# Block products of a GLA and SwiGLU layer: the last of four sums of raw weights made by an accumulating DMA instead of VectorE

## The chip, the core and the metric

The kernel runs on one core of a Trainium2 chip. The core has five engines that run their own instruction streams and wait for each other through semaphores: TensorE (PE, the matrix products; its weight loads are shown as PEld), VectorE (DVE), ScalarE (ACT), GpSimd (POOL) and SyncE (SP, which here only issues DMAs). DMAs issued by SP go through the hardware queue q1, those issued by GpSimd through the software queue q0; both are carried by the same 16 DMA engines. The metric is the device time of one execution in microseconds (us).

## The reference

One layer with 512 tokens and width 2048, in float32. Only the first kind of mixer is used (a gated linear attention, GLA), then a SwiGLU:

```python
h = rms_norm(x, norm_g[0, 0])
y = gla_mixer(h, w_in, w_a2, b_a, g_norm, w_out)   # 4 heads, ends in o @ w_out, w_out 2048 x 2048
x = x + y
x = x + swiglu(rms_norm(x, norm_g[0, 1]), w_gu, w_down)

def swiglu(h, w_gu, w_down):                       # w_gu 2048 x 11264, w_down 5632 x 2048
    g, u = split(h @ w_gu, 2)
    return (silu(g) * u) @ w_down
```

The change concerns the three last products, o @ w_out, h @ w_gu and (silu(g) * u) @ w_down.

## The kernel before, in words

**Split operands.** A float32 operand is split into hi (a rounded copy, made by ScalarE) and lo (what is left, made by VectorE), and a product is three matmuls: hi x hi, hi x lo, lo x hi (L1096 to L1098).

**Block products.** The three last products are made in the manner of Strassen and Winograd: a 2 x 2 block product takes seven products instead of eight, with sums of blocks on both sides. The activations' sums ("forms", seven a chunk: e0, e1, e2, l1, l0, e3, l2) are made once, split, and kept in DRAM or on chip; their tiles on chip are named fe and fl. The weights' sums are made on the fly from raw blocks of 256 x 512 (a tile of 128 x 1024, 512 KB): B11 (slot 0), B12 (slot 1), B22 and later B21 (both slot 2).

**Groups, phases, jobs.** The work is a list of 21 groups: groups 0 and 1 for w_out, groups 2 to 12 for w_gu, groups 13 to 20 for w_down. Each group has 2 to 4 chunks of the inner dimension and seven phases, one for each form; a job is one phase of one chunk, 12 matmuls. PHASES (L651) gives for each phase the form, the slot of the weights that is split, the bank that the product is added to, and the sum that is made first:

```python
("e0", 0, "x", None), ("e1", 0, "y", (0, 1, 0)), ("e2", 0, "x", (0, 0, 2)),
("l1", 2, "y", (1, 2, 1)), ("l0", 1, "x", None), ("e3", 2, "z", (0, 0, 2)), ("l2", 0, "x", None)
```

So phase 1 makes slot 0 = slot 1 - slot 0, phase 2 slot 0 = slot 0 - slot 2, phase 3 slot 1 = slot 2 - slot 1, and phase 5, once slot 2 holds B21, slot 0 = slot 0 + slot 2; that is what phase 6 multiplies. All four sums are made by VectorE (L687). Phases 0, 1, 2 and 6 read slot 0, phase 4 slot 1, phases 3 and 5 slot 2.

**Order.** The order on each engine is that in which the program emits its instructions. `run_job(m)` (L1070) emits the sum of job m + 3 (`add_stage`), the split of job m + 2 (`split_stage`: hi by ScalarE L696, lo by VectorE L697, into a pool of three buffers), the 12 matmuls of job m, and then what is due at m. `split_stage` also emits the loads into the buffers that a split has freed: at phase 3 the load of B21 (blk 3), at phases 4, 5 and 6 the three first loads of the next group (L675, all on SP). Among what is due (`at(m, ...)`) are, one job after a phase's last, the `take` functions that fetch the finished banks, and the form loads (L582, on SP).

**Groups 0 and 1.** `take_out` (L896) starts its sums s, v and u at phases 0, 1 and 2: ScalarE copies the bank to a tile (L915) and GpSimd issues an accumulating DMA of 256 KB that adds the residual x from DRAM to it (L916; two each, one for each half of 256 tokens). VectorE adds the later banks: to u at phase 3's take (L918), to v at phase 4's (L921), to s at phase 5's (L926); L918 is due with the first job of phase 4. GpSimd's queue also holds the stores of finished sums (L906), of forms (L603, L828), and in the down groups the loads of the residual (L1054), whose addition (L1058) is emitted three jobs later. In group 0 the forms of the last head are not ready before the group starts: the forms l1, l0 and l2 are loaded while it runs (`late_loads`, L748), the four of l0 are emitted at jobs 11 to 14, and phase 4 begins with job 16. Group 1 uses the same forms again, which are then on chip. Of the forms of group 2, those of two chunks are stored by GpSimd to DRAM (xF, L828) during groups 0 and 1 and loaded by SP in group 1; the others are made in place.

Of the kernel before, what the change touches and what calls it, by code (L numbers as in the profile page):

```python
# [11 lines left out]
ALU = mybir.AluOpType  # L12
PSUM = bass.MemoryType.PSUM

P = 128
# [9 lines left out]
G = 512  # L25
# [11 lines left out]
def f32(ap):  # L37
    return ap.bitcast(F32)
# [3 lines left out]
def trunk_kernel(ctx: ExitStack, tc: tile.TileContext, x, xT, cst, masks, wa2r, w_in, w_out, w_gu, w_down, out):  # L42
    nc = tc.nc
# [21 lines left out]
    def mis_bank():  # L65
        return mis_ps.tile([P, G], F32, tag="mis", name="mis")
# [161 lines left out]
    b = mis_bank()  # L228
# [352 lines left out]
    def load_form(src, f, c):  # L581
        nc.sync.dma_start(f32(form_tile(f, c % 4)), src[c][:, MADE.index(f)])  # L582
# [48 lines left out]
    def early_load(c):  # L631
# [15 lines left out]
    groups = [(w_out, range(4), (2 * p * G, (2 * p + 1) * G)) for p in range(2)]  # L647
    groups += [(w_gu, range(4) if fg else (0, 1, 3, 2), (fg * G, FF + fg * G)) for fg in range(N_FG)]
    groups += [(w_down, chunks, (2 * p * G, (2 * p + 1) * G)) for p, chunks in DOWN]

    PHASES = (  # L651
        ("e0", 0, "x", None),
        ("e1", 0, "y", (0, 1, 0)),
        ("e2", 0, "x", (0, 0, 2)),
        ("l1", 2, "y", (1, 2, 1)),
        ("l0", 1, "x", None),
        ("e3", 2, "z", (0, 0, 2)),
        ("l2", 0, "x", None),
    )
    jobs = [(g, ph, j) for g in range(len(groups)) for ph in range(7) for j in range(len(groups[g][1]))]  # L660
# [3 lines left out]
    w_at = {}  # L664

    def load(g, blk, j):

        if g >= len(groups) or j >= len(groups[g][1]):
            return
        src, chunks, cols = groups[g]  # L670
        slot = min(blk, 2)
        t = rw.tile([P, 2, G], F32, tag=f"r{(slot + g) % 3}{j}", name="raw")
        k0 = 4 * chunks[j] + (2 if blk > 1 else 0)
        n0 = cols[0] if blk in (0, 3) else cols[1]
        nc.sync.dma_start(t, src[k0 * P : (k0 + 2) * P, n0 : n0 + G].rearrange("(c p) f -> p c f", p=P))  # L675
        w_at[g, slot, j] = t
# [3 lines left out]
    def add_stage(m):  # L680
        if m >= len(jobs) or m in added:
            return
        added.add(m)
        g, ph, j = jobs[m]
        if (op := PHASES[ph][3]) is not None:
            to, a, b = (w_at[g, slot, j] for slot in op)
            (nc.vector.tensor_add if ph == 5 else nc.vector.tensor_sub)(to, a, b)  # L687

    def split_stage(m):
        if m >= len(jobs):  # L690
            return
        g, ph, j = jobs[m]
        raw = w_at[g, PHASES[ph][1], j]
        hi = wp.tile([P, 2, G], F32R, tag="hi", name="hi")
        lo = wp.tile([P, 2, G], F32R, tag="lo", name="lo")
        nc.scalar.copy(hi, raw)  # L696
        nc.vector.tensor_sub(lo, raw, f32(hi))  # L697
        ahead.append((hi, lo))
        split_done.append(m)
        if ph == 3:  # L700
            load(g, 3, j)
        elif ph > 3:
            load(g + 1, ph - 4, j)
            if j == len(groups[g][1]) - 1:
                for k in range(j + 1, 4):
                    load(g + 1, ph - 4, k)
# [13 lines left out]
    x1d = dram.tile([P, 4, D], F32, name="x1d")  # L720

    split_stage(0)
    split_stage(1)
    add_stage(4), add_stage(5)
    last = gate(3, banks)
    split_stage(2)
    ps.close()
    zz_ps = ffn.enter_context(tc.tile_pool(name="zz_ps", bufs=1, space=PSUM, reuse_waits="tile"))
# [15 lines left out]
    def at(m, fn):  # L744
        due.setdefault(m, []).append(fn)
# [221 lines left out]
    for n in range(2):  # L967
        for ph, k in enumerate((18, 18, 19, 19, 20, 22, 26)):
            at(first_of[1, 0] + k + n, lambda f=PHASES[ph][0], n=n: load_form(xF, f, n))

# [71 lines left out]
    def plan_loads():  # L1042
        seen = set()
        for d, (_, chunks) in enumerate(DOWN):
            for i, c in enumerate(c for c in chunks if c not in seen):
                seen.add(c)
                for ph in range(7):
                    at(first_of[D0 + d - 1, ph] + i + 1, lambda f=PHASES[ph][0], c=c: load_form(hF, f, c))

# [20 lines left out]
    def run_job(m):  # L1070
        nonlocal XYZ, keep
        g, ph, j = jobs[m]
        f, _, q, _ = PHASES[ph]
        chunks = groups[g][1]
        if j == 0:
            if ph == 0:
                XYZ, keep = dict(first_banks) if g == 0 else {}, {}
            if q not in XYZ:
                pr = banks_of["xyz".index(q)]
                XYZ[q] = [bank(f"q{pr}{i}") for i in range(2)]  # L1080
        add_stage(m + 3)
        while len(split_done) <= min(m + 2, len(jobs) - 1):
            split_stage(len(split_done))
# [94 lines left out]
```

## Time and profile before

| | us |
|---|---|
| median of 3 timed runs | 2079.57 (2078.95 to 2079.61) |
| the profiled execution, its own time | 2081.49 |
| its span in the trace | 2079.7 |
| TensorE busy in it | 2065.5 |
| VectorE, ScalarE, GpSimd busy | 1601.7, 938.7, 313.5 |
| mean granted TensorE clock | 0.997 |

The profile names an instruction by engine, line of the kernel and tiles, as out<-in. In a row of a group, the numbers behind the bar are its busy time in us and the mean of one in ns, and behind the second bar the idle time of the engine just before it and what ended that. A row of the timeline has the start and the length in us. A row of the waits has the total, the number of times and the longest. A row of busy time by windows has the length and then, for each engine, the busy time and the number of instructions, then granted clock, share of the 16 DMA engines that is busy (the shares of packets can add up to a little over 1) and GB/s. A row of a DMA queue has packets, MB and the share of the 16 engines' time in the window asked for. A "DMA to landing" is the time from the issue of a DMA to the semaphore that tells that its data are there.

### The profile page before, as it was taken

How to read it: one execution, taken by the hardware profiler on the slowest of the kernel's cores; microseconds unless marked ns; L12 is line 12 of the kernel's file. 1: busy time of each engine (PE TensorE's matmuls, PEld its weight loads, DVE VectorE, ACT ScalarE, POOL GpSimd, SP SyncE). 2: the span in 40 equal slices, each digit the busy share in tenths (PEclk: the TensorE clock that was granted, in tenths of full speed). 3: DMA queues.
4: the chain of work that ended last, by engine and by line, in shares of the span. 5: the costliest groups of instructions: out<-in, count | busy, mean ns of one | idle time of the engine just before them, and what ended most of it. 6: DMA issues, size and time to landing. Idle time of an engine off the chain costs nothing.

```text
span 2079.7 us, 24526 instructions
## 1 busy us (share of the span) xinstructions
PE 2065.5 (99%) x9314; PEld 1713.0 (82%) x9314; DVE 1601.7 (77%) x1778; ACT 938.7 (45%) x1165; POOL 313.5 (15%) x315
## 2 busy tenths in 40 slices
PE   9999999999999999999999999999999999999999
PEld 7887888888887887888888888888888888888887
DVE  7856566665448799788788788788788787888887
ACT  6343334333334556545445445445445454333333
POOL 6324242423111120011011011011011010000000
PEclk9999999999999999999999999999999999999999
DMA  6222222224784885553553553553555676675632
GB/s 212 76 83 68 78 71 81 82 77 129 261 310 141 320 264 211 164 177 114 173 178 114 174 177 114 175 177 115 173 176 167 223 278 243 223 273 194 233 136 100
DMA packets 161333, 350.22 MB, mean 168 GB/s; under 512 B 14400, under 2 KB 30912, under 8 KB 161216
## 3 DMA queue, kind: packets, MB, share of 16 engines
q1 hardware_dynamic: 136704, 274.76, 40.9%
q0 software_dynamic: 21440, 71.84, 10.2%
q10 hardware_dynamic: 3072, 2.06, 0.3%
q8 instruction: 73, 1.20, 0.2%
q14 instruction: 44, 0.36, 0.1%
HBM read 279.93 MB, written 68.68 MB: 168 GB/s over the span
## 4 chain that ended last, share of the span: by engine, by line
PE 94%; DVE 4%; ACT 1%; POOL 0%; issue 0%; DMA 0%; SPq 0%; DVEq 0%; ACTq 0%; POOLq 0%
PE bank L1097 22%; PE bank L1098 22%; PE bank L1096 22%; PE acc L134 8%; PE acc L133 8%; PE acc L135 7%; PE mis L427 2%; PE bank L791 1%; DVE lo L697 1%; DVE raw L687 1%; PE mis L485 1%; PE mis L135 0%; PE mis L133 0%; PE mis L134 0%; DVE qt L392 0%
## 5 line engine op out<-in xcount | busy, mean ns | idle before, releaser
L696 ACT CAST hi<-raw 128x1024 fp32r<-128x1024 f32 x518 | 544.5, 1054 | 684.7 <-PE bank L1098 574.9
L697 DVE TENSOR_TENSOR lo<-raw,hi 128x1024 fp32r<-128x1024 f32 x518 | 631.5, 1223 | 202.0 <-ACT hi L696 199.3
L1097 PE MATMUL bank<-lo,fe 128*128 128x512 f32 x1184 | 462.5, 391 | 2.7 <-DVE lo L697 2.6
L1096 PE MATMUL bank<-hi,fe 128*128 128x512 f32 x1184 | 464.2, 392 | 0.1
L1098 PE MATMUL bank<-hi,fe 128*128 128x512 f32 x1184 | 462.1, 390 | 0.0
L687 DVE TENSOR_TENSOR raw<-raw 128x1024 f32<-128x1024 f32 x296 | 361.0, 1220 | 2.7 <-DMA raw<-w_down 2.4
L1096 PE MATMUL bank<-hi,fl 128*128 128x512 f32 x888 | 345.7, 389 | 0.0
L1098 PE MATMUL bank<-hi,fl 128*128 128x512 f32 x888 | 345.5, 389 | 0.0
L1097 PE MATMUL bank<-lo,fl 128*128 128x512 f32 x888 | 345.5, 389 | 0.0
L1097 PEld LDWEIGHTS bank<-lo,fe 128*128 128x128 f32 x1184 | 222.8, 188 | 51.6 <-DVE lo L697 6.3
L1098 PEld LDWEIGHTS bank<-hi,fe 128*128 128x128 f32 x1184 | 222.7, 188 | 46.6
L1096 PEld LDWEIGHTS bank<-hi,fe 128*128 128x128 f32 x1184 | 222.7, 188 | 46.0 <-ACT hi L696 0.5
L122 DVE TENSOR_TENSOR lo<-raw,hi 128x1024 fp32r<-128x1024 f32 (+1 forms) x97 | 124.0, 1286 | 166.1 <-ACT hi L121 153.4
L133 PE MATMUL acc<-x,hi 128*128 128x512 f32 x512 | 202.9, 396 | 0.5 <-ACT x L170 0.5
L134 PE MATMUL acc<-x,hi 128*128 128x512 f32 x512 | 199.6, 390 | 0.3 <-DVE x L171 0.3
L135 PE MATMUL acc<-x,lo 128*128 128x512 f32 x512 | 199.7, 390 | 0.1
L121 ACT CAST hi<-raw 128x1024 fp32r<-128x1024 f32 (+1 forms) x97 | 100.6, 1040 | 213.1 <-PE acc L134 144.1
L1097 PEld LDWEIGHTS bank<-lo,fl 128*128 128x128 f32 x888 | 166.7, 188 | 35.5
L1096 PEld LDWEIGHTS bank<-hi,fl 128*128 128x128 f32 x888 | 166.7, 188 | 35.1 <-issue 0.3
L1098 PEld LDWEIGHTS bank<-hi,fl 128*128 128x128 f32 x888 | 166.7, 188 | 34.2
L828 POOL DMA_DIRECT2D hF<-hh x44 | 33.0, 749 | 788.3 <-ACT hs L818 691.9
L133 PEld LDWEIGHTS acc<-x,hi 128*128 128x128 f32 x512 | 96.2, 188 | 21.3 <-issue 1.0
(208 smaller groups left out, 2105.2 us busy)
## 6 DMA issues: line engine op xcount, KB each, us to landing
raw<-w_gu SPq DMA_DIRECT2D x176, 512.0 KB, 4.2
raw<-w_down SPq DMA_DIRECT2D x88, 512.0 KB, 5.4
raw<-w_in SPq DMA_DIRECT2D x64, 512.0 KB, 3.9
fe<-hF SPq DMA_DIRECT2D x44, 512.0 KB, 5.9
fl<-hF SPq DMA_DIRECT2D x33, 512.0 KB, 6.6
raw<-w_out SPq DMA_DIRECT2D x32, 512.0 KB, 8.5
raw<-w_in SPq DMA_DIRECT2D x62, 256.0 KB, 3.2
gF<-st POOLq DMA_DIRECT2D x48, 256.0 KB, 5.3
```

What stands on the lines that cost most here:

```text
L121: nc.scalar.copy(hi[:, c], raw[:, c])
L122: nc.vector.tensor_sub(lo[:, c], raw[:, c], f32(hi[:, c]))
L133: nc.tensor.matmul(out, ah, bh, start=start, stop=False)
L134: nc.tensor.matmul(out, ah, bl, start=False, stop=False)
L135: nc.tensor.matmul(out, al, bh, start=False, stop=stop)
L427: nc.tensor.matmul(bk[:, g * w : (g + 1) * w], kt[:, c, gg * P : (gg + 1) * P], qt[:, o : o + w], start=c == 0, stop=c == 1,)
L687: (nc.vector.tensor_add if ph == 5 else nc.vector.tensor_sub)(to, a, b)
L696: nc.scalar.copy(hi, raw)
L697: nc.vector.tensor_sub(lo, raw, f32(hi))
L1096: nc.tensor.matmul(o, ah, bh, start=a and begin, stop=False, skip_group_check=True)
L1097: nc.tensor.matmul(o, ah, bl, start=False, stop=False, skip_group_check=True)
L1098: nc.tensor.matmul(o, al, bh, start=False, stop=z, skip_group_check=True)
```

## The change

The fourth sum is no longer made by VectorE. When `split_stage` emits the split of phase 3 and the load of B21 into slot 2, it now also emits, on GpSimd's queue, a DMA that reads the same B21 block from DRAM once more and adds it to slot 0 in place (`accum_op=ALU.add`). Phase 5 keeps its split of B21 and its products, and has no sum in PHASES any more, so `add_stage` issues only subtractions.

```diff
-        ("e3", 2, "z", (0, 0, 2)),
+        ("e3", 2, "z", None),
...
-            (nc.vector.tensor_add if ph == 5 else nc.vector.tensor_sub)(to, a, b)
+            nc.vector.tensor_sub(to, a, b)
...
         if ph == 3:
             load(g, 3, j)
+            src, chunks, cols = groups[g]
+            k0 = 4 * chunks[j] + 2
+            nc.gpsimd.dma_start(
+                w_at[g, 0, j],
+                src[k0 * P : (k0 + 2) * P, cols[0] : cols[0] + G].rearrange("(c p) f -> p c f", p=P),
+                accum_op=ALU.add,
+            )
```

There are 74 such DMAs of 512 KB, one for each chunk of each group.

## The prediction

> **What bounds the kernel now.** First the page's busy times, the DMA row of the 40 slices and the group of the step that is moved.
>
> ```profile
> PE 2065.5 (99%) x9314; PEld 1713.0 (82%) x9314; DVE 1601.7 (77%) x1778; ACT 938.7 (45%) x1165; POOL 313.5 (15%) x315
> DMA  6222222224784885553553553553555676675632
> L687 DVE TENSOR_TENSOR raw<-raw 128x1024 f32<-128x1024 f32 x296 | 361.0, 1220 | 2.7 <-DMA raw<-w_down 2.4
> ```
>
> TensorE is busy 99% of a span of 2079.7 us: 14.2 us of idle time are left, in the whole kernel. VectorE, which the change relieves, is at 77%. So the next view is who waits for whom, kept to TensorE: does it ever wait for VectorE?
>
> ```profile
> PE mis L427 <- DVE qt L400: 5.3, 4, 3.0
> PE bank L1097 <- DVE lo L697: 2.6, 3, 1.6
> ```
>
> The first row is the attention stage, which the change leaves alone. In the block products TensorE waits for VectorE's splits three times, 2.6 us together. That is the most that a lighter VectorE can give back there.
>
> The third view is busy time by windows. The first two lie in the first block product group (group 0); the next two are around the largest of the three waits; then the gate/up groups, and one group of the down projection.
>
> ```profile
> 666.00:667.30 1.30, 1.30 (x7) 1.09 (x6) 1.30 (x2) 0.54 (x1) 0.00 (x0) 1.00 0.05 9
> 667.30:687.00 19.70, 19.70 (x88) 16.06 (x86) 14.17 (x14) 9.57 (x13) 2.90 (x4) 1.00 0.99 320
> 645.40:647.50 2.10, 0.55 (x2) 0.24 (x2) 2.10 (x3) 1.59 (x3) 0.00 (x0) 1.00 0.00 0
> 647.50:651.00 3.50, 3.50 (x9) 2.77 (x10) 3.47 (x5) 2.54 (x5) 2.38 (x3) 0.51 0.27 43
> 760.00:1600.00 840.00, 839.30 (x3790) 694.28 (x3789) 705.58 (x766) 429.33 (x533) 62.70 (x86) 1.00 0.53 167
> 1700.00:1757.00 57.00, 57.00 (x253) 47.19 (x253) 44.55 (x42) 26.02 (x29) 2.06 (x3) 1.00 0.80 282
> ```
>
> The last three columns are granted clock, DMA share and GB/s. From 667.3 to 687.0 the DMA engines have nothing free (0.99), while TensorE still is never idle: the two have the same length there. And a TensorE wait is followed by a stretch at half clock (0.51 for 3.5 us), which costs another 1.7 us.
>
> How near the edge that stretch is, the timelines of SP and TensorE say, with the landing times of two of SP's form loads (those issued at 671.43 and 676.47).
>
> ```profile
> 666.45 0.38 SPq L675 DMA_DIRECT2D raw<-w_out  x1
> 668.72 0.38 SPq L675 DMA_DIRECT2D raw<-w_out  x1
> 669.16 1.52 SPq L582 DMA_DIRECT2D fl<-gF  x1
> 671.43 0.46 SPq L582 DMA_DIRECT2D fl<-gF  x1
> 676.47 0.42 SPq L582 DMA_DIRECT2D fl<-gF  x1
> ```
> ```profile
> 678.88 0.39 PE L1096 MATMUL bank<-hi,fl 128*128 128x512 f32 x1
> 681.66 0.47 PE L1096 MATMUL bank<-hi,fl 128*128 128x512 f32 x1
> 687.20 0.39 PE L1096 MATMUL bank<-hi,fl 128*128 128x512 f32 x1
> ```
> ```profile
> L582 SPq DMA_DIRECT2D fl<-gF x1: 458/458/458, 671.4 to 671.4; - x1
> DMA to landing us min/median/max: 10.1/10.1/10.1
> ```
> ```profile
> L582 SPq DMA_DIRECT2D fl<-gF x1: 425/425/425, 676.5 to 676.5; - x1
> DMA to landing us min/median/max: 10.5/10.5/10.5
> ```
>
> The four loads from 669.16 on are the l0 forms of group 0, one for each job of its phase 4; the jobs begin at 678.88, 681.66, ... 687.20, so a job is 2.8 us. The second form lands at 671.4 + 10.1 = 681.5 and is used at 681.66; the fourth lands at 676.5 + 10.5 = 687.0 and is used at 687.20. The margin is 0.2 us. Whatever is put into the DMA engines ahead of these loads comes out of TensorE.
>
> **Removed.** A quarter of the 296 additions, 74 x 1.22 us = 90 us of VectorE. All are in phase 5, between phases in which VectorE has room; the 1.6 us wait at 645.4 lies in phase 1 of group 0, before any of them. Gain 0, at most 2.6 us. ScalarE's split of phase 5 now waits for the load of B21 by itself, one job (2.8 us) later than the addition did; this eases the only late load in the L687 row (2.4 us).
>
> **Added.** 74 DMAs of 512 KB from the GpSimd queue. B21 is still loaded by SP for phase 5, so this is traffic on top. The trace has accumulating DMAs of 256 KB (residual x, L916): the queue rows show what a pair, 512 KB, costs while nothing else runs (660 to 667), what plain copies cost (782 to 790), both together (674 to 681), and the five us within that in which both always had work (675 to 680).
>
> ```profile
> q0 software_dynamic: 288, 0.52, 46.8%
> ```
> ```profile
> q1 hardware_dynamic: 1047, 3.24, 102.8%
> ```
> ```profile
> q1 hardware_dynamic: 536, 1.35, 55.5%
> q0 software_dynamic: 288, 0.52, 45.4%
> ```
> ```profile
> q0 software_dynamic: 265, 0.49, 59.8%
> q1 hardware_dynamic: 326, 0.79, 45.3%
> ```
>
> Accumulating: 46.8% of 7 us = 3.28 us of all 16 engines. Plain: 102.8% of 8 us for 3.24 MB, so 1.33 us for 0.524 MB. An accumulation is 2.5 loads. GpSimd issues a pair in some 1.8 us (the v row below): 74 times that is 133 us on an engine that is busy 15%, at no cost but order. The Trainium skill (Collectives: The Full Stack, section "The bandwidth ceiling: the fold count and why AG ≠ RS ≠ AR") says a reduce needs two reads where a copy needs one and runs at half the rate; by it an accumulation would be an estimated 2.7 us and the 11.6 us below would be 9.1. The rows here say 2.5 times, and go into the sum.
>
> Together they do not overlap: 0.52 MB at 3.28 us and 1.35 MB at 3.4 us make 6.7 of the 7 us in which both were moving. Where both have work, q0 gets 59.8 of 105.1 parts, 0.57.
>
> **Where the accumulations run.** Each waits for the two reads of phase 2's split of its chunk, and follows in GpSimd's queue what the program puts before it.
>
> ```profile
> 660.42 1.80 POOL L916 DMA_DIRECT2D v<-x  x2 [2.24 <-ACT v L915]
> 670.61 1.76 POOL L916 DMA_DIRECT2D u<-x  x2 [8.39 <-ACT u L915]
> ```
>
> In group 0 the first three come after v (issued by 662.2) and before u; the fourth after u. Their data follow v's directly: they find the engines free for the 1.3 us at 666.0 (0.05 busy), then meet the full stretch. The forms wait for 4 x 3.28 - 1.3 = 11.8 us more work, less 0.2 us of margin: **+11.6 us** in group 0. If only three are served before the last form, it is 8.3; if fewer, less. The half clock that follows such waits is hidden here behind the next form's wait, and so is u of group 0, which stands in the queue with the accumulations: VectorE can be held as long as the last form is.
>
> **Group 1** uses the same forms, on chip by then, so another step is the near one: u, the accumulated residual of phase 2, which VectorE adds in phase 4 (L918) with all later splits behind it. Here u is again behind three accumulations in the same queue. GpSimd's queue, VectorE and TensorE there, with the landing of u and of the store (xF) that precedes the accumulations:
>
> ```profile
> 744.71 1.41 POOL L828 DMA_DIRECT2D xF<-hs  x1
> 753.94 1.85 POOL L916 DMA_DIRECT2D u<-x  x2 [7.81 <-ACT u L915]
> ```
> ```profile
> xF<-hs POOLq DMA_DIRECT2D x1, 512.0 KB, 7.7
> ```
> ```profile
> DMA to landing us min/median/max: 6.6/7.0/7.3
> ```
> ```profile
> 762.82 1.28 DVE L918 TENSOR_TENSOR u<-u,bank 128x512 f32<-128x512 f32 x2
> ```
> ```profile
> 750.00:770.00 20.00, 20.00 (x90) 16.54 (x89) 18.99 (x23) 11.94 (x19) 6.03 (x8) 1.00 0.94 303
> ```
> ```profile
> 767.94 0.39 PE L1096 MATMUL bank<-hi,fl 128*128 128x512 f32 x1
> ```
>
> The store issued at 744.71 landed at 752.4; I take 751 for the accumulations' first data. Three of them and u are 4 x 3.28 = 13.1 us of engine time. SP's loads of B21 and of group 2 are there too (the window 750 to 770 is at 0.94 already), so q0 gets between 0.57 of the engines and all of them; I take 0.67, near the lower end, since SP's loads of B21 come one by one at first: 13.1 / 0.67 = 19.6, u at 770.6. Then its two adds and one split (1.28 + 1.22 us) end at 773.1, where TensorE wants that split at 767.94: **+5.1 us**. With all of the engines u would land at 764.1 and cost nothing, since 766.6 is before 767.94; with 0.57 it lands at 774.0 and costs 8.6. The half clock after it adds **1.7**.
>
> Behind u in GpSimd's queue stand the last xF stores, and SP's loads of the forms of group 2 wait for those, with group 2's raw loads behind them on SP. They are all loaded a group ahead and TensorE is later too, so I cost them at nothing; without that cover they would cost what they are late.
>
> **The other groups.** What else GpSimd's queue holds there are stores for a much later stage, and the residual loads of the down groups, issued three jobs (8.4 us) ahead of the addition that uses them:
>
> ```profile
> res<-x1d POOLq DMA_DIRECT2D x16, 256.0 KB, 5.2
> ```
>
> They have 3 us to spare, and VectorE's splits another job behind that. A gate/up group has 28 jobs, 78 us: 13.1 us of accumulation lifts a DMA share of 0.53 to 0.70. A down group of three chunks: 9.8 us in 57 us lifts 0.80 to 0.97, just under full. From the split of phase 2 to that of phase 6 there are four phases, 45 us with four chunks, 22 with two: more than an accumulation with its landing. I cost these at 0, and at a few us where the 0.97 does not hold.
>
> **Sum.** 11.6 + 5.1 + 1.7 - 0 = 18.4 us. The profiled execution took 2081.49 us with a span of 2079.7; the median of the three timed runs, 2079.57, equals the span, so I add to that: **2098 us**.
>
> **Rivals.** About 4.2 us (0.2%) is what a measurement here can tell from no change.
>
> - *Only group 0, or less of it* (2084 to 2091): u gets the engines nearly alone, or the last form passes some of the accumulations. For it: in group 1 SP's loads come one by one. Against: the 0.94 there. Chance 0.27; the forecast's own case (2091 to 2106) 0.52.
> - *Not slower: the engines interleave.* An accumulating packet waits for its second read, and SP's packets use that time; the forms land as before, and the kernel gives 2077 to 2081. It decides if an accumulation takes less than 0.4 us (1.3 + 0.2 us over four) from SP's queue. For it: the share of an accumulation is long for its bytes. Against: the seven us above, where the two added up. Chance 0.14. The Trainium skill (DMA: Bandwidth & Descriptors, section "Rules for kernel authors") says that spreading DMAs over issuing engines gains no bandwidth, since all run on the same 16; by it this rival does not exist, and the rows of 674 to 681 agree.
> - *Faster*: VectorE's 90 us come through. It would need TensorE to wait for VectorE 4.2 us; it waits 2.6. Chance 0.02, at 2075.
> - *Much slower*: the down groups run full and wait in each; over 2106. Chance 0.05.
>
> **How the numbers follow.** Slower is 0.52 + 0.27 + 0.05 = 0.84, no change 0.14, faster 0.02. The range leaves out the not slower cases (0.16) and nearly all of the last: 2082 to 2108.
>
> **What would show it.** TensorE idle before L1096 and L1097 at phase 4 of group 0, on l0 forms that land 8 to 12 us later; L918 of group 1 waiting for u; granted clock of 0.5 behind both; 222 additions left in L687; q0's share up by 74 x 3.28 / 2079.6 = 12 points; from group 3 on TensorE as gapless as before. It is wrong if group 0's phase 4 has no gaps, or if the gaps lie in the down groups.

## The result and the profile after

| | before | after |
|---|---|---|
| median of 6 timed runs, us | 2079.47 (2078.45 to 2081.03) | 2092.19 (2091.2 to 2094.51) |
| ratio, 95% interval | | 1.0061 (1.0050 to 1.0072) |
| profiled execution, its own time, us | 2081.49 | 2094.31 |
| span in the trace, us | 2079.7 | 2092.5 |

The kernel became 12.7 us slower: the direction that was forecast, at two thirds of the size, and inside the range. The change did what it says. The page of after, its busy times, the DMA row of the 40 slices, the accumulating queue, the additions that are left, and the group of matmuls whose idle time grew most:

```profile
PE 2068.9 (99%) x9314; PEld 1714.4 (82%) x9314; DVE 1521.0 (73%) x1704; ACT 938.8 (45%) x1165; POOL 404.1 (19%) x389
DMA  6222222224685988763763763763765888897854
q0 software_dynamic: 41568, 110.64, 20.7%
L1104 PE MATMUL bank<-hi,fl 128*128 128x512 f32 x888 | 347.7, 392 | 6.1 <-DMA fl<-gF 6.1
L688 DVE TENSOR_TENSOR raw<-raw 128x1024 f32<-128x1024 f32 x222 | 269.8, 1215 | 0.2
```

VectorE lost 74 additions and 80.7 us, GpSimd has 74 issues and 90.6 us more, and TensorE has the same matmuls, 3.4 us more of busy time in them. So the 12.7 us are idle time and slower matmuls of TensorE. (Lines from L687 on have moved by one, those behind the new DMA by eight: the addition is L688, the split L697 and L698, the matmuls L1104 to L1106, the new DMA L705, u's residual L924 and its addition L926. In the runs further down the numbers differ again by a few; there the rows are told by their tiles.)

The rows of the waits of TensorE in after say who made it wait; the first row is the untouched attention stage, the other two are new or larger:

```profile
PE mis L427 <- DVE qt L400: 5.3, 4, 3.0
PE bank L1104 <- DMA fl<-gF: 6.1, 2, 3.6
PE bank L1105 <- DVE lo L698: 5.1, 5, 2.0
```

There are two waits for form loads, and 5.1 us of waits for VectorE's splits (2.6 before). Of these 2.5 us more, 1.98 are one wait in group 1; the rest is a wait of 0.55 us in group 0's phase 1, ahead of the accumulations, which stands in every profile but that of before. The windows show where the loss lies: the stretch of group 0 that was full before, the half-clock stretch inside it, its counterpart in group 1, then the same two windows of gate/up and down groups as before.

```profile
667.30:696.00 28.70, 22.62 (x86) 17.83 (x86) 12.21 (x12) 9.56 (x13) 4.17 (x5) 0.88 1.07 310
685.90:692.00 6.10, 6.10 (x15) 4.81 (x16) 0.00 (x0) 0.61 (x1) 0.81 (x2) 0.52 1.04 404
780.00:783.80 3.80, 3.80 (x10) 3.04 (x11) 2.36 (x2) 1.38 (x2) 0.00 (x0) 0.57 1.04 412
760.00:1600.00 840.00, 837.33 (x3774) 692.66 (x3773) 653.26 (x721) 429.09 (x534) 116.44 (x129) 1.00 0.64 194
1700.00:1757.00 57.00, 57.00 (x257) 47.31 (x256) 42.07 (x43) 27.69 (x33) 7.24 (x8) 1.00 0.97 328
```

Before, TensorE was busy in all of the 19.7 us from 667.3 to 687.0; now it is busy in 22.62 of 28.70 us. The last two rows are as gapless as before: the 840 us window lacks 2.67 us of busy time, 1.98 of them the group 1 wait at 778, and the down group has none at a DMA share of 0.97.

TensorE's timeline in after, group 0 and then group 1; in brackets the wait and what ended it:

```profile
676.43 0.39 PE L1106 MATMUL bank<-hi,fl 128*128 128x512 f32 x1
679.30 0.47 PE L1104 MATMUL bank<-hi,fl 128*128 128x512 f32 x1 [2.49 <-DMA fl<-gF]
...
681.91 0.39 PE L1106 MATMUL bank<-hi,fl 128*128 128x512 f32 x1
685.89 0.77 PE L1104 MATMUL bank<-hi,fl 128*128 128x512 f32 x1 [3.59 <-DMA fl<-gF]
...
777.57 0.39 PE L1104 MATMUL bank<-hi,fl 128*128 128x512 f32 x1
779.93 0.50 PE L1105 MATMUL bank<-lo,fl 128*128 128x512 f32 x1 [1.98 <-DVE lo L698]
```

The landings of three of SP's form loads in after, the last of l1 (issued at 667.7), the first of l0 (669.9) and the last of l0 (679.2):

```profile
L582 SPq DMA_DIRECT2D fl<-gF x1: 625/625/625, 667.7 to 667.7; - x1
...
  PE bank L1104: 2.5, 1
...
DMA to landing us min/median/max: 11.5/11.5/11.5
```
```profile
L582 SPq DMA_DIRECT2D fl<-gF x1: 547/547/547, 669.9 to 669.9; - x1
...
  PE bank L1104: 3.6, 1
...
DMA to landing us min/median/max: 15.8/15.8/15.8
```
```profile
L582 SPq DMA_DIRECT2D fl<-gF x1: 3431/3431/3431, 679.2 to 679.2; - x1
...
DMA to landing us min/median/max: 16.7/16.7/16.7
```

They land at 679.2, 685.7 and 695.9. The first two end TensorE's two waits. The last one landed at 687.0 before, so it is 8.9 us later: SP issues it 2.8 us later, and it is 6.2 us longer on its way. Nobody waits for it, because TensorE has meanwhile lost as much: 6.1 us of waits, and about 2.9 of the 6.1 us at a clock of 0.52. TensorE begins the job that uses it at 696.92:

```profile
696.92 0.39 PE L1104 MATMUL bank<-hi,fl 128*128 128x512 f32 x1
```

Without the slow stretch it would have waited for the second and third l0 forms instead, which land at 689.6 and 693.3, and would have been there some 0.9 us earlier (an estimate: 693.3 and one job of 2.8 us).

Group 1 loses its time as the prediction had it. The landing of u's residual and VectorE's timeline in after:

```profile
L924 POOL DMA_DIRECT2D u<-x x2: 885/914/943, 763.3 to 764.1; - x2
...
DMA to landing us min/median/max: 12.6/13.2/13.8
```
```profile
775.99 0.69 DVE L926 TENSOR_TENSOR u<-u,bank 128x512 f32<-128x512 f32 x1 [3.96 <-DMA u<-x]
778.05 0.69 DVE L926 TENSOR_TENSOR u<-u,bank 128x512 f32<-128x512 f32 x1 [1.38 <-DMA u<-x]
```

The landing, 6.6 to 7.3 us before, takes 12.6 to 13.8 us; VectorE stands for the second half until 778.05, the split behind it is late, and TensorE gets it at 779.93. Then come 3.8 us at a clock of 0.57, some 1.6 us lost.

Set job by job against before, TensorE is 0.5 us late already ahead of group 0's phase 3, loses 9.1 us in group 0 and 3.8 in group 1, and within 1 us nothing later on.

### The profile page after: what moved, and what is told of

Read it like the earlier page. It is cut to its first block, busy times and chain, and to the rows that moved or that the text cites. A ratio compares the mean times of both kernels' runs of the same rounds, so it can differ in the third digit from the quotient of the medians.

```text
span 2092.5 us, 24710 instructions
## 1 busy us (share of the span) xinstructions
PE 2068.9 (99%) x9314; PEld 1714.4 (82%) x9314; DVE 1521.0 (73%) x1704; ACT 938.8 (45%) x1165; POOL 404.1 (19%) x389
## 4 chain that ended last, share of the span: by engine, by line
PE 92%; DVE 4%; DMA 2%; issue 1%; POOL 1%; ACT 1%; SPq 0%; POOLq 0%; DVEq 0%; ACTq 0%
PE bank L1105 21%; PE bank L1104 21%; PE bank L1106 21%; PE acc L134 8%; PE acc L133 7%; PE acc L135 7%; PE mis L427 2%; PE bank L799 1%; DMA fl<-gF 1%; DVE lo L698 1%; DMA u<-x 1%; DVE raw L688 1%; PE mis L485 1%; PE mis L133 0%; PE mis L135 0%
## 5 line engine op out<-in xcount | busy, mean ns | idle before, releaser
L697 ACT CAST hi<-raw 128x1024 fp32r<-128x1024 f32 x518 | 544.6, 1054 | 691.9 <-PE bank L1106 575.5
L698 DVE TENSOR_TENSOR lo<-raw,hi 128x1024 fp32r<-128x1024 f32 x518 | 630.4, 1221 | 291.9 <-ACT hi L697 289.7
L1104 PE MATMUL bank<-hi,fe 128*128 128x512 f32 x1184 | 463.3, 391 | 0.1
L1106 PE MATMUL bank<-hi,fe 128*128 128x512 f32 x1184 | 461.1, 389 | 0.0
L1104 PE MATMUL bank<-hi,fl 128*128 128x512 f32 x888 | 347.7, 392 | 6.1 <-DMA fl<-gF 6.1
L1106 PE MATMUL bank<-hi,fl 128*128 128x512 f32 x888 | 347.0, 391 | 0.0
L688 DVE TENSOR_TENSOR raw<-raw 128x1024 f32<-128x1024 f32 x222 | 269.8, 1215 | 0.2
L1104 PEld LDWEIGHTS bank<-hi,fe 128*128 128x128 f32 x1184 | 222.3, 188 | 46.1 <-ACT hi L697 0.6
L1106 PEld LDWEIGHTS bank<-hi,fe 128*128 128x128 f32 x1184 | 222.2, 188 | 45.8
L1104 PEld LDWEIGHTS bank<-hi,fl 128*128 128x128 f32 x888 | 167.6, 189 | 41.8 <-issue 6.9
L1106 PEld LDWEIGHTS bank<-hi,fl 128*128 128x128 f32 x888 | 167.8, 189 | 34.7
```

Source lines behind the costliest of these rows:

```text
L688: nc.vector.tensor_sub(to, a, b)
L1104: nc.tensor.matmul(o, ah, bh, start=a and begin, stop=False, skip_group_check=True)
L1106: nc.tensor.matmul(o, al, bh, start=False, stop=z, skip_group_check=True)
```

## The experiments

Theory: all of the loss comes from eight of the 74 accumulations, those of groups 0 and 1, because there something due soon shares the full DMA engines or the queue with them. Rivals: the loss is spread over all groups; VectorE's 80.7 us are worth something and hide a larger loss; the place in the queue and not the engines' time is what costs; the transfers interleave for nothing. All runs were timed in five rounds, beside runs of the kernel before, whose median of the same rounds is given with each.

**1. No sum at all.** The new DMA is left out, the rest of the change stays.

```diff
-            src, chunks, cols = groups[g]
-            k0 = 4 * chunks[j] + 2
-            nc.gpsimd.dma_start(
...
-            )
```

> The fourth sum is left out altogether (neither VectorE nor a DMA adds B21 to slot 0, so the last product of each group uses the wrong weights). This is the gain side of the change alone. Theory (VectorE is not what TensorE waits for): 2079.5 us, at most 2.6 us less. Rival (90 us of VectorE are worth something on their own): 2075 us or less.

Measured: 2080.05 against 2080.05 us, ratio 1.0002 (0.9994 to 1.0011). The time of 74 VectorE additions is worth nothing, not even where it is given back for free. The rival falls, and with it any version of this change that could gain: this is its ceiling.

**2. to 4. By groups.** The DMA is issued in some groups only; the others keep VectorE's addition.

```diff
-        if (op := PHASES[ph][3]) is not None:
+        if (op := PHASES[ph][3]) is not None and not (ph == 5 and g >= 2):
...
         if ph == 3:
             load(g, 3, j)
+            if g >= 2:
...
```

with `g >= 2` (66 DMAs), then `g == 0` (4), then `g == 1` (4).

> The accumulating DMA in groups 2 to 20 only (66 of the 74); groups 0 and 1 keep VectorE's addition. Theory (the whole loss lies in the DMA engines of groups 0 and 1): back to 2079.5 us, within 2 us, with no wait of TensorE that the kernel before lacks. Rival (the loss is spread over all groups, more traffic everywhere): some 66/74 of 12.7 us stay, 2090 us.

> The accumulating DMA in group 0 only (4 of the 74). Theory: the waits for late forms at the end of phase 3 and the start of phase 4, with the half clock behind them, come back whole, 8 us: 2087.5 us. Rival (spread over all groups): 4/74 of 12.7 us, 2080.2 us.

> The accumulating DMA in group 1 only (4 of the 74). Theory: u lands late, VectorE stands at its addition, TensorE waits some 2 us and runs 3.4 us at half clock, 3.8 us in all: 2083.3 us. Rival (group 1's wait follows from group 0's lag): 2079.5 us.

Measured, against 2080.05: groups 2 and up 2079.53, ratio 0.9997 (0.9988 to 1.0006); group 0 alone 2087.99, 1.0038 (1.0024 to 1.0051); group 1 alone 2083.31, 1.0016 (1.0008 to 1.0025). Sixty-six of the 74 cost nothing; the four of group 0 cost 7.9 us, the four of group 1 cost 3.3. Together with the -0.5 of the others that makes 10.7 of the 12.7 us, no further off than the intervals. The waits of TensorE that before lacks or that grew, first with groups 2 and up, then with group 0 alone, then with group 1 alone:

```profile
PE bank L1105 <- DMA fl<-gF: 1.1, 2, 0.7
```
```profile
PE bank L1105 <- DMA fl<-gF: 5.9, 4, 2.8
```
```profile
PE bank L1106 <- DVE lo L698: 5.4, 5, 2.3
```

The last two are the two kinds of wait that after has, for forms and for the split behind u, each where its group has the DMAs. "Spread over all groups" falls, and so does "group 1's wait follows from group 0's lag". Two details went otherwise than expected. With groups 2 and up, TensorE waits 1.1 us for forms in group 0, where this run has no new DMA: the margin of 0.2 us there is not the same in every execution. With group 1 alone, no slow clock follows the wait of 2.29 us in the profile, so that its 3.3 us fit the expected 3.8 in size but not in all they were made of.

**5. A plain copy in its place.** The same DMA without the addition, so that slot 0 is overwritten: same queue, same place, same bytes brought in.

```diff
-                accum_op=ALU.add,
```

> All 74 DMAs stay in their place in GpSimd's queue, but as plain copies: slot 0 is overwritten with B21 instead of added to, so phase 6 multiplies B21 alone. Same instructions, same order, same waits; only the second read and the addition in the DMA engines are gone. Theory (time of the DMA engines is the price): 4 x 1.33 - 1.3 - 0.2 = 3.8 us in group 0, the half clock perhaps on top, nothing in group 1: 2082 to 2085 us. Rival (the place in GpSimd's queue, or the wait for phase 2's split, is the price): 2092 us.

Measured: 2085.0, ratio 1.0024 (1.0014 to 1.0035), 5.2 us over its 2079.8. Its waits of TensorE:

```profile
PE bank L1103 <- DMA fl<-gF: 3.7, 3, 3.0
PE bank L1104 <- DVE lo L698: 3.2, 4, 1.6
```

What the same queue moved from 667 to 670, where these copies ran all but alone, says what one of them takes:

```profile
q0 software_dynamic: 311, 1.10, 95.8%
```

That is 1.4 us for 0.524 MB. At some half of the engine time for a DMA, less is lost in group 0 (3.7 us of waits against 6.1) and the four waits for splits are those of run 1 (3.2 us there too): no wait for u is left. The place in the queue is that of after, so it is not what costs by itself; the time in the engines is. The addition itself is worth 7.5 of the 12.7 us.

**6. Two of group 0.** As run 3, with `g == 0 and j < 2`.

> The accumulating DMA for the first two of the four chunks of group 0 only; VectorE adds the rest. Theory (the forms are late by the engine time put ahead of them): an accumulation at the rate seen in the changed kernel while nothing else moved (0.61 MB in 3 us, 2.6 us each) gives 2 x 2.6 - 1.3 - 0.2 = 3.7 us: 2083.5 us. Rival (only the accumulations that run beside the loads cost, and the first two are nearly over by then): 2080 us.

Measured: 2082.45 against 2078.95, 3.5 us, ratio 1.0017 (1.0008 to 1.0026). In group 0 the loss goes by the number of accumulations after the free 1.3 us are used up: two 3.5, four 7.9.

**7. Group 0 with earlier loads.** The l0 forms are emitted four jobs earlier, with those of l1.

```diff
-                at(m + (0, 4, 11)[i] + n, lambda f=f, n=n: load_form(gF, f, n))
+                at(m + (0, 0, 11)[i] + n, lambda f=f, n=n: load_form(gF, f, n))
```

> The change whole, with the l0 forms of group 0 loaded together with the l1 forms, four jobs earlier, for three of the four chunks into idle DMA time before group 0. Theory (forms that land late are what TensorE waits for in group 0): the 3.6 us wait for the first l0 form goes, the 2.5 us one for the last l1 form stays, with a half clock behind it: 2088 to 2089 us. Rival (the loads of B21 or u are late as well and take over): 2092 us.

Measured: 2086.56 against 2079.8, 6.8 us, where after has 12.7; ratio 1.0037 (1.0025 to 1.0050). Its waits of TensorE:

```profile
PE bank L1104 <- DMA fl<-gF: 2.7, 1, 2.7
PE bank L1105 <- DVE lo L698: 5.1, 5, 2.0
```

One of the two form waits is gone, with the slow clock behind it; the other, and u's in group 1, are as in after. In this profile no slow clock follows these two either, which would explain that the time is 1.4 us under the 2088 expected at least. So it is the due times of these loads that turn engine time into lost time.

**8. Earlier accumulations.** They are emitted with the split of phase 2, as soon as it has read slot 0, instead of phase 3's.

```diff
-        if ph == 3:
-            load(g, 3, j)
+        if ph == 2:
             src, chunks, cols = groups[g]
...
+        elif ph == 3:
+            load(g, 3, j)
```

> All 74 accumulations, but emitted with the split of phase 2 that they wait for, not one phase later, so that they can use the time in which the DMA engines stand idle ahead of phase 3 (660 to 662 and 739 to 744 in the kernel before). Theory: group 0 gets 2 us of idle time more, its loss falls from 8 to some 5.5; in group 1 three accumulations are done before u is issued and its loss is gone: 2085 us. Rival (the amount of traffic counts, not where it lies): 2092 us.

Measured: 2096.72 against 2079.8, ratio 1.0081 (1.0069 to 1.0094), with executions from 2091.95 to 2099.75: a gain on after was expected, and it is rather slower (1.0050 to 1.0072 there). Its waits of TensorE, and ScalarE's timeline in group 1:

```profile
PE bank L1105 <- ACT hi L697: 7.0, 1, 7.0
PE bank L1105 <- DMA fl<-gF: 5.8, 2, 3.1
```
```profile
765.65 1.21 ACT L566 ACTIVATE hh<-bank,c_sb 128x256 fp32r<-128x256 f32 x3 [9.67 <-DMA xF<-hh]
```

Part of what was expected is there: job by job, group 0 loses 7.7 us instead of 9.1, and the wait for u in group 1 is gone. But now the four accumulations and v stand ahead of the two stores of forms (xF) that precede u in GpSimd's queue. These take 12.6 and 13.7 us to land, the tile hh is not free before the first has landed, ScalarE stands 9.67 us for it with the next split behind, and TensorE 7.0 us, with a slow clock after that. The expectation had not looked at what else stands in the queue.

**9. Group 1's accumulations behind u.** Group 0 as in after; `accumulate(g, j)` issues the same DMA.

```diff
...
+            if g == 1:
+                at(first_of[1, 3] + 1 + j, lambda: accumulate(g, j))
+            else:
+                accumulate(g, j)
```

> The change whole, but in group 1 the four accumulations are emitted behind u in GpSimd's queue (one job each from the second job of phase 3 on). Theory (u behind three accumulations in one queue is group 1's loss): 3.8 us come back, 2088.4 us. Rival (the engines are as full either way, so u is as late): 2092 us.

Measured: 2096.16 against 2079.8, ratio 1.0082 (1.0069 to 1.0094): a miss too, 7.8 us over what was expected. u itself is on time (6.9 to 7.9 us to landing), and TensorE does not wait for it. A row of SP's waits, and the timelines of SP, VectorE and TensorE, show the next thing in the queue:

```profile
SPq L582 <- DMA xF<-hs: 8.3, 1, 8.3
```
```profile
801.59 0.33 SPq L938 DMA_DIRECT2D piece<-x  x1
```
```profile
811.78 1.36 DVE L944 TENSOR_TENSOR w<-piece,bank 128x512 f32<-128x512 f32 x2 [6.33 <-DMA piece<-x]
```
```profile
812.62 1.49 PE L805 MATMUL bank<-c_sb,w 128*128 128x128 f32 x4 [4.45 <-DVE w L944]
```

The last xF store stands behind two of the accumulations and takes 16.5 us to land, SP's load of those forms waits 8.3 us for it, and everything that SP emits later is late with it: a piece of the residual goes out at 801.59 (782.55 before, and TensorE itself is only some 8 us later there), VectorE waits 6.33 us for it and TensorE 4.45, with a clock of 0.57 from 812 to 816. In after the last xF stores take 18 us and more as well, and the same piece goes out at 800.24. But there VectorE comes to it at 811.25, against 805.45 here, for the most part because of the wait for u, and finds it landed. So the wait for u had covered the next one.

**10. and 11. Parts of group 1.** As run 4, with only the last of the four (`j == 3`, emitted behind u), and with only the first three (`j < 3`, ahead of u).

> The accumulating DMA for the last chunk of group 1 only, which stands behind u in GpSimd's queue. Theory (u is late by what stands ahead of it in its own queue): 2079.5 us. Rival (u is late because the engines are shared while it moves): 1 us or more, 2081 us.

> The accumulating DMA for the first three chunks of group 1 only, which stand ahead of u. Theory (u is late by what stands ahead of it): the whole loss of group 1, 2083.3 us. Rival (all four share the engines with u): three quarters of it or less, 2082 us.

Measured, against 2078.95: the last alone 2079.06, ratio 0.9997 (0.9989 to 1.0006), nothing; the first three 2080.65, ratio 1.0010 (1.0001 to 1.0018), 1.7 us, half of what the four of run 4 cost, with executions from 2078.69 to 2085.83. TensorE's timeline with three:

```profile
766.72 0.50 PE L1106 MATMUL bank<-lo,fl 128*128 128x512 f32 x1 [2.00 <-DVE lo L698]
```

The whole wait for u, 2 us, is there with the three ahead of it alone, and none with the one behind it. By time the theory for three missed: it expected the whole loss, and half of it is what the rival allowed. The intervals of the two runs overlap, so whether the 1.6 us between them are real is open. The profiles suggest where they could come from: with all four, in run 4 and in run 7, a piece of work at 803 us was late as well (in run 4 TensorE waits 0.30 us, then 0.29, about 1 us lost), which the profiles of three and of the last alone do not show.

## Why the prediction was right, and where it was off

**Bound and removed work: right.** TensorE at 99% and 2.6 us of waits for VectorE said that a lighter VectorE gives nothing; run 1 shows none, to within its interval.

**Groups 2 and up: right.** The gate/up share rose from 0.53 to 0.64 (0.70 forecast), the down share from 0.80 to the 0.97 forecast, without a gap; run 2 shows none. q0's share of the span rose by 10.5 points (12 forecast).

**Group 0, 11.6 us: right mechanism, one term too large.** What failed is the term 3.28 us for one accumulation. It was the packet time of one pair of 256 KB. The queue rows of after from 664 to 667.3, which is nearly all v's pair, the kind that the price was taken from, and from 668 to 671, where nothing but the new accumulations ran, have

```profile
q0 software_dynamic: 223, 0.40, 97.9%
```
```profile
q0 software_dynamic: 317, 0.61, 111.4%
q1 hardware_dynamic: 3, 0.01, 0.6%
```

The second is 0.61 MB in 3 us, so 2.6 us for 0.524 MB by elapsed time, and 2.9 by packet time, because shares add up to over 1. The first would be 4.3 us by elapsed time, at a share of 0.98. So v's pair was no measure for the accumulations behind it; why it is slower, no run here shows. With 2.6 the same sum is 4 x 2.6 - 1.3 - 0.2 = 8.9 us, the 8.9 us by which the last form is late, and 9.1 were lost; for two accumulations it gives 3.7, and 3.5 were measured (run 6). The Trainium skill (Collectives: The Full Stack, section "The bandwidth ceiling: the fold count and why AG ≠ RS ≠ AR") gives a reduce half the rate of a copy, and by it the prediction had worked out 9.1: 2.6 us against 1.3 (SP's loads before) and 1.4 (run 5's copies) side with the page.

**"The half clock is hidden in group 0": wrong in its working.** It was to lie behind the next form's wait. In after it took the place of those waits: only two of the forms are waited for, and about 2.9 us go at a clock of 0.52. That the total still fits is in part luck: the last form landed at 695.9, and TensorE came to it 1 us after that, held up by the slow clock and not by the form. The first late form was also not one of l0, as assumed, but the last of l1.

**Group 1, 5.1 + 1.7 us: right place and mechanism, the wait too large.** It is u, behind three accumulations (runs 10 and 11). Two estimates were off against each other: 2.6 us each instead of 3.28, and less of the engines than the 0.67 taken. Seen from before, TensorE being 9.6 us later, u was whole at 777.9 - 9.6 = 768.3 instead of 770.6; four times 2.6 us from 751 on gives a share of 10.4 / 17.3 = 0.60. The row of 672 to 676 in after, with both queues at work, has nearly the same:

```profile
q0 software_dynamic: 262, 0.50, 68.0%
q1 hardware_dynamic: 263, 0.57, 42.2%
```

68.0 of 110.2 parts are 0.62, half-way between the prediction's lower end and its choice. That makes 2.3 of the 3.1 us. The rest is that u comes in halves: the first addition was done when the second landed, and TensorE waited 2.0 us, not 5.1. The slow clock behind it cost 1.6 us in the profile of after, as forecast; in the profiles of runs 4, 7 and 11 it did not come, so it is no fixed price, and that it came here is luck.

**"xF stores behind u cost nothing": right, but with little cover.** In after SP waits 3.5 us for the last of these stores before it can load those forms, and nobody is late. Where the accumulations stand ahead of the earlier stores too (run 8), this cost TensorE 7.0 us, and where it was no longer late through u itself (run 9), 4.45.

**The rivals.** "Interleave" falls: in the full stretch the shares of both queues add up to 1.1 and the forms land 8.9 us later. "Only group 0, or less of it" falls with run 4, but narrowly: its range ended at 2091, and without group 1's 3.3 us the time would lie in it. "Faster" falls with run 1, "much slower" with run 2. The sum of 18.4 us was too large by 5.7: 2.5 in group 0 by the term of one accumulation, 3.1 in group 1's wait.

## What to carry to other kernels

Before putting more traffic on DMA engines that are busy half of the time on average, look for the stretches where they are full and read the margin between landing and use there: 8 of 74 transfers cost all of the 12.7 us. Price a transfer in a stretch that it fills alone, by bytes over elapsed time, and in more than one such stretch: here 512 KB of accumulation took 2.6 us in one and 4.3 in another, and the share of packet time counts overlap twice. A transfer that is moved to spare one user of its queue meets the next one, and a wait that is taken away uncovers the next: list all that stands behind it, stores whose tiles are to be freed among them.

## What the runs showed of the hardware

- An accumulating DMA of 512 KB took 2.6 us of all engines from 668 to 671 in after; v's pair of 256 KB just ahead, 664 to 667.3, moved at a rate of 4.3 us for 512 KB. A plain one took 1.3 us on SP's queue (3.24 MB in 8 us before) and 1.4 us on GpSimd's (run 5). All are by elapsed time. The issue of an accumulating one costs GpSimd 90.6 / 74 = 1.22 us on average.
- While accumulations filled the engines, SP's queue moved next to nothing: its loads issued at 667.2 and 667.7 are in the 668 to 671 window with 0.01 MB. Later both share, at 0.62 to 0.38. SP's issues themselves stretch, to 3.43 us for the form load at 679.2 (0.42 before).
- A wait of TensorE of 3.59 us was followed by 6.1 us at a clock of 0.52 and one of 1.98 us by 3.8 us at 0.57, but one of 2.49 us in the same execution, the 2.29 and 2.00 us of runs 4 and 11, and even one of 2.98 us in run 5 (clock 1.00 from 683 to 690) by matmuls at full speed. The 1.55 us wait in group 0's phase 1, behind which the prediction saw 3.5 us at 0.51, stands in all thirteen profiles, and in before alone the clock was slow after it. TensorE's timeline right behind that wait in after, and right behind the wait for u in run 4:

```profile
648.21 0.50 PE L1105 MATMUL bank<-lo,fe 128*128 128x512 f32 x1 [1.54 <-DVE lo L698]
648.55 0.40 PE L1106 MATMUL bank<-hi,fe 128*128 128x512 f32 x1
```
```profile
771.03 0.50 PE L1106 MATMUL bank<-lo,fl 128*128 128x512 f32 x1 [2.29 <-DVE lo L698]
771.37 0.40 PE L1107 MATMUL bank<-hi,fl 128*128 128x512 f32 x1
```

The Trainium skill (TensorE: Matmul & The Clock Gate, section "What's actually happening") has the slow clock come after at least one idle window of some 3.4 us, in windows that run free of the program. The wait of 3.59 us fits that. The 1.98 us wait is shorter and was followed by the slow clock all the same; no run tested what decides, and it stays open.
